# A hybrid decoder layer on one core: the gate columns of its input projection, from one product per tile and half to pairs of tiles with seven block products over both halves

## The chip, the core and the metric

The kernel runs on one core of one Trainium2 chip. TensorE (PE) multiplies matrices into PSUM; VectorE (DVE), ScalarE (ACT) and GpSimd (POOL) do the elementwise work, GpSimd without access to PSUM; SyncE (SP) issues most of the transfers between the chip's memory and SBUF, POOL and ACT issue the others. The metric is the device time of one launch in microseconds (us), lower is better.

## The reference, cut to what matters

```python
h = rms_norm(x, norm_w)                       # x (1024 positions, 2048)
proj = h @ w_in                               # 8704 columns
q, k, v, a_gate, u, z, g_a, g_s = jnp.split(proj, split_pts, axis=-1)   # a_gate, u, z 1024 wide; g_a, g_s 2048
attn = sliding_window_attention(rms(q), rms(k), v, sinks)               # window 128
y_a = (attn * jax.nn.silu(a_gate)) @ w_attn_proj
y_ssm = jax.nn.gelu(s5_ssm(u, ...))           # a diagonal complex scan over the positions
glu_a, glu_b = jnp.split(y_ssm @ w_glu + b_glu, 2, axis=-1)
y_s = (glu_a * jax.nn.sigmoid(glu_b) * jax.nn.silu(z)) @ w_ssm_proj
merged = jax.nn.sigmoid(g_a) * y_a + jax.nn.sigmoid(g_s) * y_s
return x + merged @ w_out
```

The gate columns are `a_gate`, `z`, `g_a` and `g_s`: 6144 of the 8704. All data are fp32.

## The kernel before, in words

Everything is held transposed: channels on the 128 partitions, positions along the free axis, in two halves of 512 positions (h = 0 and 1; `TH` is 512). A weight tile `win(n)` is 2048 rows by 128 columns and is loaded as two blocks of 8 x 128 rows (`wraw`, 128x1024 elements, 512 KB). For fp32 accuracy every operand is split into a rounded part and a rest: `split` (lines 81 and 82) makes `hi` by a copy on ACT and `lo` by a subtraction on DVE. A block product takes 8 row tiles of 128, three matmuls for each (hi by hi, hi by lo, lo by hi): 24 matmuls of 128x128 by 128x512, added up in one PSUM bank.

The input projection has 68 weight tiles: 0 to 11 for k, v and q, 12 to 19 for u, 20 to 27 for z (`gate`), 28 to 35 for the attention gate (`gate` with `by`), 36 to 51 for g_a and 52 to 67 for g_s (`sigmoids`). `proj` (line 111) makes each tile for each half by itself, so a tile costs two block products per half, four in all, and its weights are loaded and split twice. A gate's bank is multiplied with `rstd` on DVE (L176, L186), goes through the sigmoid on ACT (L177, L187) and is stored by POOL's queue (L178, L193). `build_raw` makes the split operand `hh`/`hl` of a half: 16 pairs of an ACT and a DVE instruction (L143, L144).

The later products (GLU, attention output, SSM output, final output) already use a scheme with seven block products for the eight of a 2 x 2 block matrix. For GLU, attention and SSM `four` does it for a pair of weight tiles; for the final output `out1`, `out2`, `out3` do it in three walks over the tiles, with intermediate results in memory. Sums of weight blocks are made by `wadd` on POOL (L856).

Work is emitted by generators: `drive` runs one and, after each of its steps, `pull` advances the side generators in `sides` by their rate (`spawn(gen, rate)`); `drain` finishes them. A scheduler then orders the instructions of each engine by priority on its own estimate of when they become ready, and each engine and each queue runs its list in order. Tiles with one tag of a pool share its `bufs` buffers; a tile waits until one is free. The split weights have two buffers, the loaded blocks (`raw`) two.

The order of the stages: u and z of half 0 beside the SSM's tables (`ssm_prep`); k, v, q of half 0; u, k, v, q of half 1 beside attention of half 0; z and half of g_a of half 1 beside attention of half 1; the other gates of half 1, then a_gate and g_a of half 0, beside `ssm` (the scan: in four batches of 16 groups, each with DVE steps in `step`, POOL products of its tables, L661, and px and py matmuls, L706, L753, L754); g_s of half 0 beside the input sums of the GLU; then the later products.

The shape of the scheme in the kernel before, for one product of the second walk of the final output:

```python
r1, r2, r3 = rring(wout(8 + j, 0)), rring(wout(8 + j, 1)), rring(wout(j, 0))
w1, w2 = wsum(), wsum()
wadd(w1, r1, r2)
wadd(w2, r3, w1)
t = wsplit(w2)
y = bank(1)
product(y, t, 0, ops[6])
```

## Time and profile before

| what | value |
|---|---|
| time, median of 3 runs | 2614.22 us (2613.48 to 2615.66) |
| profiled execution: time, span | 2613.01 us, 2611.2 us |
| mean granted TensorE clock | 0.981 |
| busy: PE, DVE, ACT, POOL | 2480.6, 1654.7, 916.9, 917.3 us |
| PE instructions (matmuls and transposes) | 11012 |
| bytes moved, mean rate | 438.55 MB, 168 GB/s |

The span is from the first to the last instruction. A busy share is an average over stages of different kinds; the windows by stage show them apart. A granted clock below 1 is a mean over stretches at 2.4 GHz and at 1.2 GHz. DVE, ACT and POOL times count instructions from start to end, waits for a shared memory port among them.

### The profile page before, as it was taken

How to read it: one execution, taken by the hardware profiler on the slowest of the kernel's cores; microseconds unless marked ns; L12 is line 12 of the kernel's file. 1: busy time of each engine (PE TensorE's matmuls, PEld its weight loads, DVE VectorE, ACT ScalarE, POOL GpSimd, SP SyncE). 2: the span in 40 equal slices, each digit the busy share in tenths (PEclk: the TensorE clock that was granted, in tenths of full speed). 3: DMA queues.
4: the chain of work that ended last, by engine and by line, in shares of the span. 5: the costliest groups of instructions: out<-in, count | busy, mean ns of one | idle time of the engine just before them, and what ended most of it. 6: DMA issues, size and time to landing. Idle time of an engine off the chain costs nothing. (4 is left out here: it accounts for less than half of the span.)

```text
span 2611.2 us, 30785 instructions
## 1 busy us (share of the span) xinstructions
PE 2480.6 (95%) x11012; PEld 2016.8 (77%) x11012; DVE 1654.7 (63%) x2294; ACT 916.9 (35%) x1378; POOL 917.3 (35%) x715
## 2 busy tenths in 40 slices
PE   7999999999999998899999989999999999899997
PEld 5878887788878777787777868887877877678886
DVE  7995557984776287948586243226687686744542
ACT  5332454453666223131332232223352231233311
POOL 4110014350444534132120230004547656514466
PEclk9999999999999998999999999999999999999999
DMA  6543343223333745445464674336358677797765
GB/s 206 191 139 109 96 141 105 84 83 97 97 95 103 217 129 135 152 129 157 133 168 135 210 259 156 121 121 202 120 191 282 211 257 234 246 313 270 226 218 181
DMA packets 195609, 438.55 MB, mean 168 GB/s; under 512 B 41312, under 2 KB 53632, under 8 KB 195456
## 3 DMA queue, kind: packets, MB, share of 16 engines
q1 hardware_dynamic: 159680, 344.14, 43.6%
q0 software_dynamic: 19504, 63.08, 6.4%
q10 hardware_dynamic: 16272, 29.38, 2.9%
q8 instruction: 86, 1.41, 0.2%
q14 instruction: 67, 0.55, 0.1%
HBM read 341.73 MB, written 94.77 MB: 167 GB/s over the span
## 5 line engine op out<-in xcount | busy, mean ns | idle before, releaser
L121 PE MATMUL ps<-hh,whi 128*128 128x512 f32 x2144 | 851.3, 397 | 13.7 <-ACT whi L81 9.7
L122 PE MATMUL ps<-hl,whi 128*128 128x512 f32 x2144 | 844.5, 394 | 0.8 <-DVE hl L144 0.8
L82 DVE TENSOR_TENSOR wlo<-wraw,whi 128x1024 fp32r<-128x1024 f32 (+1 forms) x344 | 448.6, 1306 | 455.3 <-ACT whi L81 216.9
L125 PE MATMUL ps<-hh,wlo 128*128 128x512 f32 x2144 | 549.8, 396 | 32.0 <-DVE wlo L82 32.0
L81 ACT CAST whi<-wraw 128x1024 fp32r<-128x1024 f32 (+1 forms) x344 | 348.4, 1014 | 627.4 <-PE ps L122 301.3
L125 PEld LDWEIGHTS ps<-hh,wlo 128*128 128x128 f32 x2144 | 404.7, 190 | 124.6 <-DVE wlo L82 39.5
L121 PEld LDWEIGHTS ps<-hh,whi 128*128 128x128 f32 x2144 | 407.2, 190 | 108.5 <-ACT whi L81 17.1
L122 PEld LDWEIGHTS ps<-hl,whi 128*128 128x128 f32 x2144 | 407.1, 190 | 86.7 <-DVE hl L144 2.1
L82 DVE TENSOR_TENSOR wlo<-ws,whi 128x1024 fp32r<-128x1024 f32 x80 | 118.9, 1488 | 127.1 <-ACT whi L81 93.7
L81 ACT CAST whi<-ws 128x1024 fp32r<-128x1024 f32 x80 | 84.0, 1051 | 307.5 <-POOL ws L856 116.7
L856 POOL TENSOR_TENSOR ws<-wraw 128x512 f32<-128x512 f32 (+1 forms) x72 | 136.5, 1896 | 135.6 <-DVE wlo L82 103.3
L421 POOL TENSOR_TENSOR pa<-ph,c_mct 128x512 fp32r<-128x512 f32 x32 | 43.1, 1347 | 253.8 <-ACT ph L81 253.6
L178 POOL DMA_DIRECT2D gsd<-sg x32 | 17.5, 547 | 274.9 <-ACT sg L177 274.9
L177 ACT ACTIVATE sg<-sg 128x512 f32<-128x512 f32 x64 | 40.5, 632 | 198.1 <-DVE sg L176 198.0
L661 DVE TENSOR_TENSOR v<-X,be 64x16 f32<-64x16 f32 (+2 forms) x192 | 91.9, 479 | 2.8
L402 ACT ACTIVATE scs<-scs,m,rq 128x128 f32<-128x128 f32 x128 | 61.8, 484 | 63.9 <-DVE m L396 63.9
L1001 POOL TENSOR_TENSOR mt<-mt,pa 128x512 f32<-128x512 f32 x32 | 57.0, 1782 | 76.9 <-DMA pa<-pd 24.3
L178 POOL DMA_DIRECT2D gd<-sg x32 | 17.8, 556 | 170.6 <-ACT sg L177 163.5
L862 PE MATMUL psm<-q4h,whi 128*128 128x512 f32 x160 | 67.6, 422 | 4.0 <-DVE mt L996 2.7
L862 PE MATMUL psm<-q1h,whi 128*128 128x512 f32 x160 | 64.4, 403 | 6.1 <-ACT whi L81 6.1
L863 PE MATMUL psm<-q4l,whi 128*128 128x512 f32 x160 | 66.2, 414 | 0.0
L862 PE MATMUL psm<-q2h,whi 128*128 128x512 f32 x160 | 62.6, 392 | 3.1 <-ACT qa L893 3.1
(343 smaller groups left out, 4187.8 us busy)
## 6 DMA issues: line engine op xcount, KB each, us to landing
wraw<-w_in SPq DMA_DIRECT2D x268, 512.0 KB, 3.6
wraw<-w_out SPq DMA_DIRECT2D x72, 512.0 KB, 5.2
x<-xT SPq DMA_DIRECT2D x96, 256.0 KB, 4.0
gd<-sg POOLq DMA_DIRECT2D x32, 256.0 KB, 3.9
gsd<-sg POOLq DMA_DIRECT2D x32, 256.0 KB, 2.9
wraw<-w_glu SPq DMA_DIRECT2D x16, 512.0 KB, 4.3
wraw<-w_attn SPq DMA_DIRECT2D x16, 512.0 KB, 5.1
sga<-gd SPq DMA_DIRECT2D x32, 256.0 KB, 4.3
```

The source lines that it names most:

```text
L81: S.copy(hi, src)
L82: V.tensor_tensor(lo, src if src2 is None else src2, hi.bitcast(F32), op=ALU.subtract)
L121: PE.matmul(ps, hi[:, kk, :], rh[kt], start=(kt == 0), stop=False)
L122: PE.matmul(ps, hi[:, kk, :], rl[kt], start=False, stop=False)
L125: PE.matmul(ps, lo[:, kk, :], rh[kt], start=False, stop=(kt == last))
L402: S.activation(sc[:, r, :], sc[:, r, :], AF.Exp, bias=m4[:, r:r + 1], scale=RQ[h, p][:, b, 2 * r + e:2 * r + e + 1], accum_out=den[:, r:r ...
L421: G.tensor_tensor(a, ph.bitcast(F32), mb, op=ALU.mult)
L661: (eng or V).tensor_tensor(o, a, b, op=op)
L856: G.tensor_tensor(o, a, b, op=ADD)
L862: PE.matmul(ps, hi[:, c0 + k, :], rh, start=(first and k == 0), stop=False, skip_group_check=True)
L863: PE.matmul(ps, hi[:, c0 + k, :], rl, start=False, stop=False, skip_group_check=True)
L1001: G.tensor_tensor(t, t, p, op=ADD)
```

## The change

All 48 gate tiles are made in 24 pairs of tiles (`PAIRS`; kinds a = g_a, s = g_s, z, o = a_gate) over both halves at once, with seven block products to a pair, in three walks over the pairs. The products of a walk use operands that are the same for all pairs, so each walk holds only two or three of the seven operands (eight split row tiles each). The operands that are sums over halves and row blocks are made by `inputs`, from x normalised anew, and stored in `HD`; `operands` loads and splits them. Walk 1 writes `QG[0]`, walk 2 reads it and writes `QG[1]` and `QG[2]`, walk 3 reads these. The weights of walk 2 and 3 are sums of blocks, made in place in the loaded blocks by POOL.

Half 1 goes first now: the prologue and `uproj(1)` use half 1, then half 0's operands are built (`build_raw(0)`), then u, k, v, q of half 0. Half 1's operands are then built with `rstd` in them (`build_h`), and its banks are copied or go to the sigmoid without a factor. The first eight pairs of walk 1 run ahead of k, v, q of half 1 beside attention of half 0, twelve more beside attention of half 1 and `inputs`, the last four beside the start of the SSM. The SSM runs beside walk 2 and twenty pairs of walk 3, with one buffer each for uq, X, ct, c1, c2 and the scan's temporaries, and with tables of 16 groups instead of 64. The loaded blocks get four buffers in one pool (`RAW`), where `rring` took two from each of two pools. The sums of the GLU's inputs run beside pairs 20 to 22 of walk 3, its operands are loaded beside pair 23, and the sums of the attention gate's inputs move beside the GLU.

```diff
+RAW = 4
+    HD = dp.tile([5, 8, 128, TH], F32, name="hd")
+    QG = [dp.tile([24, 128, TH], F32, name=f"qg{n}") for n in range(3)]
-        raw = wp.tile([128, KC, 128], F32, tag="raw", name="wraw")
+        raw = wp.tile([128, KC, 128], F32, tag="raw", bufs=RAW, name="wraw")
...
     def evac(ps, out, h):
-        V.tensor_tensor(out, ps, rstd[h], op=ALU.mult)
+        if h:
+            S.copy(out, ps)
+        else:
+            V.tensor_tensor(out, ps, rstd[h], op=ALU.mult)
...
-            uq = tl((128, GB, NCH), "uq", 2)
+            uq = tl((128, GB, NCH), "uq", 1)
-            X = tl((128, GB, NCH + 1), "X", 2)
+            X = tl((128, GB, NCH + 1), "X", 1)
-                v1 = tl((128, 840), f"v1{bt % 2}")[:, 0:n]
+                v1 = tl((128, 840), "v1")[:, 0:n]
...
+    PAIRS = ([("a", j, 36 + j, 44 + j, j, 8 + j) for j in range(8)] +
+             [("s", j, 52 + j, 60 + j, j, 8 + j) for j in range(8)] +
+             [("z", j, 20 + j, 24 + j, j, 4 + j) for j in range(4)] +
+             [("o", j, 28 + j, 32 + j, j, 4 + j) for j in range(4)])
+    def inputs():
+        def block(k, h, tag):
+            t = load_x(k, h, tag=tag)
+            V.scalar_tensor_tensor(t, t, nw[:, k:k + 1], rstd[h], op0=ALU.mult, op1=ALU.mult)
+            return t
+        for k in range(8):
+            b12, b11 = block(k, 0, "x"), block(k, 1, "x")
+            G.tensor_tensor(b11, b11, b12, op=SUB)
+            nc.gpsimd.dma_start(HD[0, k], b11)
+            yield
+            b22 = block(8 + k, 0, "ld")
+            nc.sync.dma_start(HD[4, k], b22)
+            G.tensor_tensor(b12, b12, b22, op=SUB)
+            nc.gpsimd.dma_start(HD[2, k], b12)
+            G.tensor_tensor(b11, b11, b22, op=ADD)
+            nc.gpsimd.dma_start(HD[1, k], b11)
+            yield
+            b21 = block(8 + k, 1, "ld")
+            G.tensor_tensor(b21, b21, b11, op=SUB)
+            nc.gpsimd.dma_start(HD[3, k], b21)
+            yield
+    def gate(kind, n, h, ps, op=None, other=None):
+        dst = {"a": GD, "s": GSD, "z": ZD, "o": AGD}[kind][h][n]
+        x = ps
+        if op is not None:
+            x = et("gx")
+            V.tensor_tensor(x, ps, other, op=op)
+        if kind in "as":
+            sg = et("sg") if op is None else x
+            S.activation(sg, x, AF.Sigmoid)
+        else:
+            sg = et("sg")
+            S.activation(sg, x, AF.Sigmoid)
+            V.tensor_tensor(sg, x, sg, op=MUL)
+            if kind == "o":
+                o = ld(AOD[h][n], "go")
+                G.tensor_tensor(sg, sg, o, op=MUL)
+        nc.gpsimd.dma_start(dst, sg)
+    def gates1(ops, a, b):
+        for p in range(a, b):
+            kind, _, na, nb, ia, ib = PAIRS[p]
+            with tc.high_priority(offset=200):
+                t1 = wsplit(rring(wq(na, 0)))
+            x = bank(0)
+            product(x, t1, 0, ops[1])
+            q = et("qa")
+            S.copy(q, x)
+            nc.gpsimd.dma_start(QG[0][p], q)
+            yield
+            with tc.high_priority(offset=200):
+                t2 = wsplit(rring(wq(na, 1)))
+            product(x, t2, 0, ops[2], first=False)
+            gate(kind, ia, 1, x)
+            yield
+    def gates2(ops, a, b):
+        for p in range(a, b):
+            kind, _, na, nb, ia, ib = PAIRS[p]
+            q = ld(QG[0][p], "qa")
+            with tc.high_priority(offset=200):
+                w5, r, w6 = rring(wq(nb, 0)), rring(wq(nb, 1)), rring(wq(na, 0))
+                wadd(w5, w5, r)
+                wadd(w6, w6, w5)
+                t = wsplit(w6)
+            y = bank(0)
+            product(y, t, 0, ops[6])
+            v = et("qb")
+            V.tensor_tensor(v, q, y, op=SUB)
+            nc.gpsimd.dma_start(QG[1][p], v)
+            yield
+            with tc.high_priority(offset=200):
+                t = wsplit(w5)
+            y = bank(0)
+            product(y, t, 0, ops[5])
+            e = et("qe")
+            V.tensor_tensor(e, y, v, op=ADD)
+            nc.gpsimd.dma_start(QG[2][p], e)
+            yield
+    def gates3(ops, a, b):
...
+                    w[7], r, w[4], w[3] = rring(wq(na, 0)), rring(wq(nb, 0)), rring(wq(nb, 1)), rring(wq(na, 1))
+                    wadd(w[7], w[7], r)
...
+                    wadd(w[3], w[3], w[4])
+                    wadd(w[3], w[3], w[7])
+                    t = wsplit(w[3])
+                y = bank(0)
+                product(y, t, 0, ops[3])
+                gate(kind, ia, 0, y, ADD, e)
...
+            product(z, t, 0, ops[7])
+            gate(kind, ib, 0, z, SUB, e)
...
+            product(z, t, 0, ops[4], first=False)
+            gate(kind, ib, 1, z, SUB, v)
...
-    spawn(stats1(), 1.0)
+    spawn(stats0(), 1.4)
     spawn(ssm_prep(b0, p0), 1.0)
-    drive(uproj(0, hh0, hl0, done, 4))
-    drive(gate(20, ZD[0], hh0, hl0, rstd[0]))
+    drive(uproj(1, hh0, hl0, done, 4))
+    hh, hl = build_raw(0)
+    drive(uproj(0, hh, hl))
...
-    drive(kvq(0, hh0, hl0))
+    drive(kvq(0, hh, hl))
     spawn(attention(0), 2.2)
-    hh, hl = build_raw(1)
-    drive(uproj(1, hh, hl))
+    hh, hl = build_h(1)
+    hu = list(zip(hh, hl))
+    og = {1: hu[0:8], 2: hu[8:16]}
+    drive(gates1(og, 0, 8))
     drive(kvq(1, hh, hl))
     drain()
-    spawn(attention(1), 2.2)
-    drive(gate(20, ZD[1], hh, hl, rstd[1]))
-    drive(sigmoids(36, GD[1], hh, hl, rstd[1], 0, 8))
+    spawn(attention(1), 2.8)
+    spawn(inputs(), 1.0)
+    drive(gates1(og, 8, 20))
     drain()
...
-    spawn(ssm(bp, pp), 0.8)
-    drive(sigmoids(36, GD[1], hh, hl, rstd[1], 8, 16))
-    drive(gate(28, AGD[1], hh, hl, rstd[1], AOD[1]))
-    drive(sigmoids(52, GSD[1], hh, hl, rstd[1], 0, 16))
-    hh, hl = build_raw(0)
-    drive(gate(28, AGD[0], hh, hl, rstd[0], AOD[0]))
-    drive(sigmoids(36, GD[0], hh, hl, rstd[0], 0, 16))
+    spawn(ssm(bp, pp), 0.7)
+    operands((6,), 1.5)
+    drive(gates1(og, 20, 23))
+    drain2()
+    operands((5,), 4.0)
+    drive(gates1(og, 23, 24))
+    drain2()
+    operands((3,), 1.5)
+    drive(gates2(og, 0, 23))
+    drain2()
+    operands((7, 4), 4.0)
+    drive(gates2(og, 23, 24))
+    drain2()
+    drive(gates3(og, 0, 20))
     drain()
...
     spawn(combos(By, CBD["y"], 4), 0.5)
-    drive(sigmoids(52, GSD[0], hh, hl, rstd[0], 0, 8))
+    drive(gates3(og, 20, 23))
     drain()
-    spawn(load_ops(oy, source(By, CBD["y"]), 4, ORDER), 0.5)
-    spawn(combos(Ba, CBD["a"], 4), 0.3)
-    drive(sigmoids(52, GSD[0], hh, hl, rstd[0], 8, 16))
+    n = load_ops(oy, source(By, CBD["y"]), 4, ORDER)
+    next(n)
+    spawn(n, 5.0)
+    drive(gates3(og, 23, 24))
     drain()
+    spawn(combos(Ba, CBD["a"], 4), 0.2)
     stage(glu, oy, load_ops(oa, source(Ba, CBD["a"]), 4, ORDER))
```

## Rows read from the trace of the kernel before

**Rows 1.** Page: busy time, share of the span, instructions of PE and DVE.

```profile
PE 2480.6 (95%) x11012; PEld 2016.8 (77%) x11012; DVE 1654.7 (63%) x2294; ACT 916.9 (35%) x1378; POOL 917.3 (35%) x715
```

**Rows 2.** Windows: length, busy us (instructions) PE PEld DVE ACT POOL, clock, DMA share, GB/s.

```profile
605.00:851.00 246.00, 241.95 (x1130) 197.41 (x1129) 165.08 (x240) 149.28 (x282) 98.33 (x83) 0.99 0.31 99
851.00:1594.00 743.00, 681.72 (x3072) 558.08 (x3071) 452.30 (x726) 206.71 (x247) 206.19 (x169) 0.97 0.56 167
1594.00:1780.00 186.00, 186.00 (x823) 154.12 (x822) 59.39 (x58) 48.42 (x54) 16.79 (x22) 1.00 0.38 121
2300.00:2612.00 312.00, 296.50 (x1296) 243.93 (x1295) 137.36 (x142) 79.58 (x100) 156.38 (x98) 0.98 0.72 240
```

**Rows 3.** Tile sg on DVE, 1594 to 1780: count, ns min/median/max, first and last start.

```profile
L176 DVE TENSOR_TENSOR sg<-ps,rstd x18: 678/684/685, 1594.4 to 1779.8; 128x512 f32<-128x512 f32 x18
```

**Rows 4.** PE's waits, 851 to 1594: us in total, times, longest.

```profile
PE ps L125 <- DVE wlo L82: 32.0, 15, 4.8
PE px L706 <- POOL bm L661: 13.0, 2, 6.5
```

**Rows 5.** Groups of instructions by form, whole span: busy us, mean ns, idle before.

```profile
L856 POOL TENSOR_TENSOR ws<-wraw 128x1024 f32<-128x1024 f32 x24 | 61.3, 2554 | 60.6 <-DVE wlo L82 28.3 <-DMA qb<-qd 12.6 <-DMA wraw<-w_out 7.9
L856 POOL TENSOR_TENSOR ws<-ws 128x1024 f32<-128x1024 f32 x8 | 19.4, 2430 | 0.2
L856 POOL TENSOR_TENSOR ws<-wraw,ws 128x1024 f32<-128x1024 f32 x8 | 19.1, 2393 | 22.2 <-issue 14.7 <-DMA wraw<-w_out 3.8 <-DVE wlo L82 3.6
L81 ACT CAST whi<-wraw 128x1024 fp32r<-128x1024 f32 x316 | 331.2, 1049 | 574.5 <-PE ps L122 301.3 <-DMA wraw<-w_in 137.9 <-PE psm L863 37.5
```

**Rows 6.** The same on POOL, 851 to 1594.

```profile
L661 POOL TENSOR_TENSOR bm<-bm,bmu 128x512 f32<-128x512 f32 x16 | 25.4, 1587 | 0.5
...
L178 POOL DMA_DIRECT2D gd<-sg x24 | 13.3, 552 | 128.7 <-ACT sg L177 121.7 <-issue 7.0
...
L661 POOL TENSOR_TENSOR bmu<-pwi,bim 128x512 f32<-128x512 f32 x8 | 12.2, 1523 | 13.0 <-DMA bim<-sBiT 7.9 <-DMA bre<-sBrT 5.0
```

**Rows 7.** The same on DVE, 851 to 1594.

```profile
L82 DVE TENSOR_TENSOR wlo<-wraw,whi 128x1024 fp32r<-128x1024 f32 x113 | 158.9, 1408 | 179.3 <-ACT whi L81 105.7 <-PE ps L125 62.4 <-DMA c<-sC 7.0
L661 DVE TENSOR_TENSOR v<-X,be 64x256 f32<-64x256 f32 x56 | 44.3, 790 | 0.8
...
L661 DVE TENSOR_TENSOR v<-v,v 128x840 f32<-128x840 f32 x8 | 8.2, 1024 | 0.0
```

**Rows 8.** DVE's timeline at the first scan: start us, us, engine line.

```profile
929.57 3.02 DVE L661 TENSOR_TENSOR v<-X,be 64x256 f32<-64x256 f32 x2
...
934.00 2.06 DVE L661 TENSOR_TENSOR X<-X,v 128x256 f32<-128x256 f32 x1
...
942.51 1.28 DVE L661 TENSOR_TENSOR v<-X,be 64x256 f32<-64x256 f32 x2
...
944.29 0.67 DVE L661 TENSOR_TENSOR X<-X,v 128x256 f32<-128x256 f32 x1
```

**Rows 9.** POOL's timeline there: the last of six table products, and what follows it.

```profile
937.14 1.46 POOL L661 TENSOR_TENSOR bm<-bm,bmu 128x512 f32<-128x512 f32 x1
950.10 0.58 POOL L178 DMA_DIRECT2D gd<-sg  x1 [11.50 <-ACT sg L177]
```

**Rows 10.** Windows: eight of 100 us with DVE over 70%; two of them, their sum.

```profile
2000.00:2100.00 100.00, 99.39 (x437) 81.41 (x436) 70.42 (x77) 30.57 (x41) 59.38 (x43) 1.00 0.74 238
...
2200.00:2300.00 100.00, 85.52 (x341) 67.28 (x340) 71.56 (x81) 27.07 (x37) 52.84 (x33) 0.93 0.77 248
sum 800.00, PE 731.86 PEld 591.33 DVE 619.35 ACT 234.47 POOL 344.31; mean PE 91.48 PEld 73.92 DVE 77.42 ACT 29.31 POOL 43.04
```

**Rows 11.** Groups on POOL, 605 to 851.

```profile
L421 POOL TENSOR_TENSOR pa<-ph,c_mpt 128x512 fp32r<-128x512 f32 x16 | 23.5, 1468 | 0.0
```

**Rows 12.** DMA issues: KB each, median us from issue to landing.

```profile
wraw<-w_in SPq DMA_DIRECT2D x268, 512.0 KB, 3.6
```

**Rows 13.** Groups on DVE, 335 to 375.

```profile
L144 DVE SCALAR_TENSOR_TENSOR hl<-x,nw,hh 128x512 fp32r<-128x512 f32 x16 | 11.4, 746 | 8.0 <-ACT hh L143 8.0
```

More of the change, by code (lines that the diff above doesn't have):

```diff
@@ L1130, in drain, with drain2 @@
         sides.clear()
+    def drain2():
+        for s in list(sides):
+            if s[2] >= 1.5:
+                for _ in s[0]:
+                    pass
+                sides.remove(s)
     def drive(gen):
```

154 lines of the change are left out of this document (87 added, 67 removed).

## The prediction, on record before the changed kernel ran

> **What bounds the kernel now.** I read the page's busy line first: PE is busy 95% of the span, no other engine over 63% [rows 1], so the count of matmuls is what has to fall. Then the windows by stage, to see where PE is not at its limit. From 1594 to 1780, with no side work, PE is busy all the time at granted clock 1.00 [rows 2], and the 18 evacuations of that stage start from 1594.4 to 1779.8 [rows 3]: 17 steps in 185.4 us, 10.91 us for two block products, **5.453 us for a product of 24 matmuls**. Next the stage beside the SSM, 851 to 1594: 56 tiles, 112 products, 610.7 us of its 743. PE is idle for 743 - 681.7 = 61.3 us there and the clock is 0.97 [rows 2], some 22 us; the remaining 49 us are the SSM's own matmuls. The waits of PE in it are mostly for the rest of the weight split, on DVE, and for the SSM's table products on POOL [rows 4]. So there is one bound, PE, and one stage that loses 83 us (61 + 22) to its helpers.
>
> **The matmuls removed.** The 48 gate tiles take 48 x 4 = 192 products, the 24 pairs take 24 x 7 = 168. 24 products less, 576 matmuls: 24 x 5.453 = **-130.9 us**. This comes off PE's own path, nothing covers it, and it is the whole of what the change can win outside the waits. The rest asks how much the helpers take back.
>
> **The walks beside the SSM.** It now stands beside 4 pairs of walk 1, all of walk 2 and 20 pairs of walk 3: 8 + 48 + 60 = 116 products, 632.5 us, and with its own 49 us 681.5.
>
> POOL: two sums for a pair in walk 2, three in walk 3, 108 here, of 128x1024. The three groups of such sums mean 2.495 us [rows 5], so 269 us. The SSM's tables are eight groups from 25.4 down to 12.2 us, 138 in all [rows 6]. Stores: 12 + 48 + 60 = 120 at 0.552 us [rows 6], 66. With the four products with the attention's output some 7. That is 480 of 681.5, 70%, where POOL had 206 of 743, 28% [rows 2].
>
> DVE: 116 splits at 1.408 us, 163; 108 banks combined at 0.684 [rows 3], 74; 16 gate products at the same, 11; the split of 40 operand tiles, each half as large as a weight split, 0.7, so 28; the SSM's steps, twelve groups from 44.3 down to 8.2 us, 211 [rows 7]. 487 us, 71%; before, 452 of 743, 61% [rows 2].
>
> So both helpers are nearer their limit while PE gives them less time. What this costs PE can only be bounded. Nearest from below is the final output, which makes the same sums in the same three walks without an SSM: it loses 15.5 of 312 us and 2% of the clock [rows 2], 7%, 48 us here. The eight windows of 100 us in which DVE is over 70% busy, as it will be, lose 8.5% of PE on the mean, and their clocks lie from 0.93 to 1.00 [rows 10]; with 3.5% for that, 12%: 681.5 / 0.88 = 774, 93 us. The worst of them loses 14.5% and 7% [rows 10]: 681.5 / 0.785 = 868, 187 us. I take 105, a little above the mean, because POOL was at 43% in the eight on the mean and will be at 70%. Against 83 before: **+22** (-35 to +104).
>
> SSM with single buffers: a batch's uq and X are loaded and cleared only when the batch before has made its last py matmul. Side steps come slower too (0.7 for 0.8 of a product), 116 x 0.7 = 81 steps for some 70 needed, so there are about 16 products, 87 us, of reserve before the drain, and then 12 products that need nothing of the SSM. I cost it at nothing; its price if that is gone is the remaining scan beyond 87 + 65 us.
>
> SP's queue: walk 3 issues four blocks and two intermediate tiles for 3 products, 2.6 MB in 16.4 us, 160 GB/s, about the 167 that this stage moved already [rows 2], at 3.6 us from issue to landing [rows 12]. Four buffers of raw blocks instead of two start them earlier. Nothing. On POOL's queue a store now waits for its sigmoid or combination with sums behind it; POOL stood idle 128.7 us in front of 24 stores [rows 6], so this waiting takes time that the sums want. It is inside the 105.
>
> **Walk 1 beside attention of half 1.** Before, 32 products (174.5 us) and 71.5 us of attention and waits made 246 [rows 2]; now 24 products, so 202 us. POOL: attention's mask products are four groups like the one shown, 88 us together [rows 11]; `inputs` adds 32 sums of about 1.55 us (one of that size on POOL is 1.587 [rows 6]), 50, and 32 stores, 18; the gates' 24 stores 13, attention's 5: 174 of 202. DVE: 165 [rows 2] less 8 splits (10) and all the products with `rstd` (18), plus 32 normalising instructions of 0.746 [rows 13] to 1.0 us, say 28: 165, 82%. Sigmoids and exponentials already shared ACT in this stage, at 61% [rows 2]. The cover if this runs late is the 8 products of pairs 20 to 23, 44 us, that need nothing of it; without that cover the 12% of above would take 202 / 0.88 - 202 = 28. Less the 5 us lost in this stage now: 0 to +23, I take **+8**.
>
> **Building half 1.** Half 1's operands take two DVE instructions for each tile, 0.746 [rows 13] and about 0.7, so 23 us where 12 stood. PE can only start on what is built: 0 to +11, I take **+6**. The new build of half 0 between the two u projections replaces one that stood in the SSM's stage. In exchange, walk 1 loses its DVE evacuations, which were hidden.
>
> **Entry into the GLU.** Its 28 operand tiles (7.3 MB, 30 us at the final stage's 240 GB/s [rows 2]; 20 us of DVE) must now be loaded in pair 23, 16.4 us, and during the first GLU tile, 19 us; they had 16 products before. Sums of the attention gate's inputs come beside the GLU as well. 0 to +20; I take **+10**. The order of the halves, the second build and the side rates of the first stages otherwise move equal work.
>
> **Sum.** -130.9 + 22 + 8 + 6 + 10 = -85. The profiled execution took 2613.0, its span 2611.2; the median of the runs is 1.2 above it. 2613.0 - 85 + 1.2 = **2529 us**.
>
> **Rivals.**
>
> *Nothing is given back* (chance 0.22). The sums of walk 2 and 3 have the form that the final output's have, where PE is busy 95%; four raw buffers prefetch deeper; and the 13 us for POOL's tables and the loss in the SSM's stage may shrink when the scan is spread thinner. With the other terms at zero and the stage's loss the same it is 2614 - 131 = 2483; at the lower bound 2450. Against it: a busier POOL beside the same scan.
>
> *Contention makes DVE the bound of the walks* (0.18). While POOL makes its table products, two scan instructions take 3.02 us and one 2.06; with POOL silent after 938.6 the same take 1.28 and 0.67 [rows 8, 9], 5.08 against 1.95, 2.6 times. POOL's sums and tables cover 407 of 681.5 us, 60%. The 256-wide steps, four groups of which the longest is shown [rows 7], 101 us together, were taken mostly with POOL silent; at 60% cover the factor 1 + 0.6 x 1.6 = 1.96 makes them 198 at most. The splits and wide steps have less to lose, some 40. DVE then needs 487 + 97 + 40 = 624, and at the 77.4% at which it ran in the eight windows [rows 10] the stage is 806, at 71.6% 872: 125 to 190 us lost, where 83 were. With 24 of other terms, 2614 - 131 + 42 + 24 = 2549, up to 2614, middle 2582. For it speaks that the sums are moved onto the one engine that slows the scan; against it, that 2000 to 2100 holds 59% of POOL and 70% of DVE with PE at 99.4% [rows 10].
>
> The Trainium skill (GPSIMD Engine Reference, 1. Specifications) says that GpSimd's SBUF interfaces are shared with VectorE and contend with VectorE instructions that have two SBUF inputs. By that rule every split and scan step is exposed, and the slower end of this rival is the likelier; the trace agrees on the scan, with 2.06 against 0.67 us.
>
> *Walk 2's chain becomes the bound* (0.15), which is slower than before. Place: sums are made in the raw blocks themselves, so a block is held until it is split, and a pair needs three of four. If buffers come free in turn, the second load of a pair waits for the split of the pair before: 1.05 [rows 5] + 1.41 us [rows 7], then the load 3.6 [rows 12], two sums 5.0, and ACT's half of the split 1.05: 12.1 us where a pair has 10.9. 1.2 us for a pair, and with a table product of POOL (1.5 to 2.7 us) ahead of each sum up to 5.4. 24 x 5.4 = 130 us: 2614 - 131 + 46 + 130 = 2659. It decides from (131 - 46) / 24 = 3.5 us for a pair. Against it: if a load takes whichever buffer is free, the third load starts 3 us before the product of sums, its sums are done 3 us into it, and the split has until the next such product, 6 us of slack.
>
> **Chances and range.** Forecast 0.45 (2505 to 2555), the three rivals 0.22, 0.18 and 0.15. The range for 8 in 10 goes from **2470 to 2612**: below it lies the lower end of the first rival, above it the third. A measurement of this kernel tells 0.2%, 5 us, from no change. Faster by more: 0.45 + 0.22 + 0.17 of the second rival = 0.84; within: 0.03, from the edges of the second and third; slower: 0.13.
>
> **What would show it.** PE's instructions fall by 576 to 10436. Products in walks with no stall are 10.9 us for two. In the walks beside the SSM, DVE over 70% and POOL near 70% busy, PE's waits led by wlo on DVE; the 256-wide scan groups well over the 790 ns of [rows 7] if contention is real. Were waits for whi behind POOL sums to lead in walk 2, at a steady step over 12 us for a pair, the chain rival holds. PE idle at the end of the stage with scan steps alone would show that single buffers cost what I put at nothing. A time under 2490 would say that helpers had room that my 71% and 70% deny; over 2610, that one of them is the bound.

## The result and the profile after

The changed kernel takes **2741.98 us** (median of 4 runs, 2740.12 to 2750.47) against 2614.94 (4 runs, 2613.48 to 2617.65): a ratio of **1.049**, 95% interval 1.0467 to 1.0515. It is slower by 127 us where 85 us less were forecast, and the time lies outside the range (2470 to 2612). All rows of the kernel after are from the longest of its four executions, 2750.47 us.

The page's busy line answers to [rows 1]. PE's instructions fell by exactly 576 and its busy time by 51 us, but its share fell from 95% to 88%; DVE rose by 227 us, POOL by 418. The columns are busy time, share of the span and instructions.

```profile
PE 2429.5 (88%) x10436; PEld 1956.9 (71%) x10436; DVE 1882.0 (68%) x2354; ACT 929.2 (34%) x1428; POOL 1334.9 (49%) x987
```

The windows by stage of the kernel after (columns as in [rows 2]): first stages; the keys, values and queries of half 0; walk 1 beside attention of half 0; its rest beside attention of half 1; walks 2 and 3 beside the SSM; the entry into the GLU; the rest.

```profile
0.00:240.00 240.00, 211.62 (x931) 165.73 (x932) 194.00 (x319) 87.62 (x124) 58.10 (x67) 0.95 0.56 182
240.00:400.00 160.00, 148.49 (x650) 121.44 (x648) 91.91 (x150) 64.79 (x121) 7.96 (x6) 0.92 0.25 79
400.00:760.00 360.00, 310.19 (x1312) 244.48 (x1312) 270.51 (x360) 174.08 (x343) 164.42 (x146) 0.89 0.44 143
760.00:991.00 231.00, 209.76 (x938) 169.17 (x937) 128.57 (x169) 120.94 (x222) 119.56 (x109) 0.95 0.43 139
991.00:1740.00 749.00, 601.63 (x2570) 487.01 (x2571) 550.38 (x699) 178.84 (x216) 405.53 (x248) 0.90 0.59 178
1740.00:1940.00 200.00, 175.88 (x729) 141.18 (x728) 120.13 (x115) 62.53 (x86) 124.91 (x95) 0.93 0.77 253
1940.00:2749.00 809.00, 771.92 (x3312) 627.84 (x3311) 526.51 (x547) 240.35 (x319) 454.42 (x318) 0.98 0.73 240
```

The stage beside the SSM is as long as before (749 us for 743 in [rows 2]) with 502 matmuls less in it. PE is idle there for 147 us instead of 61, and the granted clock is 0.90 instead of 0.97. Lower stretches come behind waits: after the wait of 11.6 us at 147 (below) the clock granted from 151 to 164 was 0.50, that is 1.2 GHz. No helper is full: DVE 73%, POOL 54%. The stage is also not the one that was planned: the last four pairs of walk 1 ran before 991, and some five of its pairs of walk 3 come after 1740, so it holds 93 products instead of 116.

To add idle time and clock without counting anything twice, I took from the trace, for every matmul, the time to the start of the next one, less the median of that time for its line and shape, and summed these differences by stage. In us:

| stage (before / after) | before | after | more | forecast |
|---|---|---|---|---|
| first stages, 0 to 240 | 16 | 36 | +20 | 0 |
| 240 to 851 / 240 to 991: attention, building half 1, walk 1 | 28 | 131 | +103 | +14 |
| beside the SSM, 851 to 1594 / 991 to 1740 | 90 | 204 | +114 | +22 |
| to the GLU, 1594 to 1780 / 1740 to 1940 | 0 | 35 | +35 | +10 |
| the rest | 58 | 51 | -7 | 0 |
| sum | 192 | 456 | +264 | +46 |

264 - 131 for the matmuls removed = +133; the spans differ by 2748.7 - 2611.2 = 137.5. So the table accounts for the result, and no term of it is a PE instruction. Two terms of the same size make most of it: the stage beside the SSM loses 92 us more than was forecast, the stages of attention 89 more.

Who is waited for in the largest term: PE's waits in 991 to 1740 (us in total, times, longest), to be read against [rows 4], where wlo had 32.0 us.

```profile
PE psm L855 <- DVE wlo L86: 64.1, 21, 8.0
PE psm L852 <- ACT whi L85: 63.6, 14, 13.1
PE py L737 <- DMA p<-ptd: 8.6, 1, 8.6
PE py L737 <- DMA c<-sC: 7.4, 1, 7.4
```

In the kernel before, whi had 9.7 us (851 to 1594):

```profile
PE ps L121 <- ACT whi L81: 9.7, 6, 3.8
```

And the DVE groups that answer to [rows 7], in the same stretch (busy us, mean ns, idle before): the split's mean went from 1408 to 1783 ns, the 64x256 scan step from 790 to 974.

```profile
L86 DVE TENSOR_TENSOR wlo<-wraw,whi 128x1024 fp32r<-128x1024 f32 x93 | 165.7, 1783 | 153.3 <-ACT whi L85 88.3 <-PE psm L855 53.9 <-issue 7.2
L644 DVE TENSOR_TENSOR v<-X,be 64x256 f32<-64x256 f32 x56 | 54.6, 974 | 0.8
L644 DVE TENSOR_TENSOR v<-X,be 64x16 f32<-64x16 f32 x120 | 34.2, 285 | 1.7
```

A mean hides how this comes about. The same splits in the kernel before (851 to 1594), the kernel after (991 to 1740) and c1 (below; 851 to 1682): ns min/median/max, first and last start.

```profile
L82 DVE TENSOR_TENSOR wlo<-wraw,whi x113: 1204/1225/3300, 849.4 to 1593.2; 128x1024 fp32r<-128x1024 f32 x113
L86 DVE TENSOR_TENSOR wlo<-wraw,whi x93: 1203/1225/9475, 1004.9 to 1736.1; 128x1024 fp32r<-128x1024 f32 x93
L82 DVE TENSOR_TENSOR wlo<-wraw,whi x114: 1208/1226/16632, 854.0 to 1680.9; 128x1024 fp32r<-128x1024 f32 x114
```

Half of the splits take 1.2 us as ever, and a few take very long. I sorted them by whether a sum or table product of POOL ran during them: in the kernel after, the 47 without one take at most 1.24 us, the 46 with one 2.36 us on the mean. The scan's steps fare the same, and a split stands behind them in DVE's order. One of PE's longest waits for wlo (start us, us; the hi part was ready at 1034.36):

```profile
1037.40 2.41 POOL L846 TENSOR_TENSOR wraw<-wraw 128x1024 f32<-128x1024 f32 x1
1037.55 3.88 DVE L644 TENSOR_TENSOR v<-X,al 128x256 f32<-128x256 f32 x1
1039.76 1.27 POOL L644 TENSOR_TENSOR bm<-bm,bmu 128x512 f32<-128x512 f32 x1
...
1043.81 0.61 DVE L644 TENSOR_TENSOR v<-X,al 128x256 f32<-128x256 f32 x1
...
1046.29 1.22 DVE L86 TENSOR_TENSOR wlo<-wraw,whi 128x1024 fp32r<-128x1024 f32 x1
1047.56 3.78 PE L855 MATMUL psm<-q6h,wlo 128*128 128x512 f32 x8 [7.46 <-DVE wlo L86]
```

The scan step that takes 0.61 us alone starts just behind a sum and ends 0.4 us after POOL's two instructions, at 1041.43; the split that PE waits for takes its usual time and starts late. Of PE's 21 waits for wlo most are of this kind: the splits that ended them are over their 1.2 us by 19 us in all, and the waits are 64. From the end of the hi part to the start of the rest 2.4 us pass on the mean in the kernel before, 4.9 in the kernel after, 3.6 in c1 and 0.6 in a3, where there is no scan (waits for a free buffer among them).

An evacuation, which has one input in PSUM, keeps its time beside the same sums:

```profile
L1142 DVE TENSOR_TENSOR gx<-psm,qe x29: 673/679/684, 1420.2 to 1737.2; 128x512 f32<-128x512 f32 x29
```

The POOL group that is new there, by which the experiments go on:

```profile
L846 POOL TENSOR_TENSOR wraw<-wraw 128x1024 f32<-128x1024 f32 x93 | 237.1, 2550 | 207.3 <-DMA wraw<-w_in 153.0 <-DVE gx L1142 16.3 <-issue 10.3
```

### The profile page after: what moved, and what is told of

The parts are those of the page before. It is cut to its first block, busy times and chain, and to the rows that moved or that the text cites. A ratio compares the mean times of both kernels' runs of the same rounds, so it can differ in the third digit from the quotient of the medians.

```text
span 2748.7 us, 30805 instructions
## 1 busy us (share of the span) xinstructions
PE 2429.5 (88%) x10436; PEld 1956.9 (71%) x10436; DVE 1882.0 (68%) x2354; ACT 929.2 (34%) x1428; POOL 1334.9 (49%) x987
## 5 line engine op out<-in xcount | busy, mean ns | idle before, releaser
L846 POOL TENSOR_TENSOR wraw<-wraw 128x1024 f32<-128x1024 f32 x120 | 304.1, 2535 | 229.7 <-DMA wraw<-w_in 171.0
L125 PE MATMUL ps<-hh,whi 128*128 128x512 f32 x608 | 242.8, 400 | 13.0 <-DVE ut L185 11.6
L126 PE MATMUL ps<-hl,whi 128*128 128x512 f32 x608 | 242.5, 399 | 3.8 <-DVE hl L148 3.8
L852 PE MATMUL psm<-hh,whi 128*128 128x512 f32 x384 | 158.8, 413 | 5.3 <-ACT qa L1166 4.0
L853 PE MATMUL psm<-hl,whi 128*128 128x512 f32 x384 | 156.6, 408 | 2.9 <-DVE hl L86 2.9
L129 PE MATMUL ps<-hh,wlo 128*128 128x512 f32 x608 | 157.0, 396 | 0.2 <-DVE wlo L86 0.2
L125 PEld LDWEIGHTS ps<-hh,whi 128*128 128x128 f32 x608 | 116.9, 192 | 39.0 <-issue 12.3
L126 PEld LDWEIGHTS ps<-hl,whi 128*128 128x128 f32 x608 | 116.9, 192 | 32.5 <-DVE hl L148 7.1
L852 PE MATMUL psm<-q7h,whi 128*128 128x512 f32 x352 | 137.3, 390 | 1.9 <-ACT whi L85 1.9
L129 PEld LDWEIGHTS ps<-hh,wlo 128*128 128x128 f32 x608 | 115.5, 191 | 25.7 <-DVE wlo L86 0.6
```

What stands on the lines that cost most here:

```text
L125: PE.matmul(ps, hi[:, kk, :], rh[kt], start=(kt == 0), stop=False)
L126: PE.matmul(ps, hi[:, kk, :], rl[kt], start=False, stop=False)
L129: PE.matmul(ps, lo[:, kk, :], rh[kt], start=False, stop=(kt == last))
L846: G.tensor_tensor(o, a, b, op=ADD)
L852: PE.matmul(ps, hi[:, c0 + k, :], rh, start=(first and k == 0), stop=False, skip_group_check=True)
L853: PE.matmul(ps, hi[:, c0 + k, :], rl, start=False, stop=False, skip_group_check=True)
```

## Experiments

Theory: POOL's sums slow DVE's scan and splits. Rivals: a chain from block to sum to split to product; single SSM buffers and the new order; DVE's amount of work. Apart from that, what the attention stages and the first stages lose. All are variants of the kernel after but one, of the kernel before. Times are single runs unless told. One kernel's runs lie up to 16 us apart (seven runs of the kernel before beside f1), and the kernel before took 2607 to 2621 us beside the single runs, so a difference under some 16 us between single runs decides nothing.

**Sums left out (a1).** The products take the loaded blocks as they are.

```
-                wadd(w5, w5, r)
-                wadd(w6, w6, w5)
...
-                    wadd(w[7], w[7], r)
...
-                    wadd(w[3], w[3], w[4])
-                    wadd(w[3], w[3], w[7])
```

> The weight sums of walk 2 and 3 are left out; the blocks are loaded and the products take them unsummed. The changed kernel lost about 200 us in walk 2 and 3 beside the SSM (991 to 1740). Theory 'sums' (the chain of load, sum, split in one set of four buffers, or POOL's sums slowing VectorE): the time falls by 90 to 150 us, to 2590 to 2650. Rival 'scan' (VectorE is too full with the SSM's steps and two evacuations for each pair, whoever makes the sums): it falls by less than 40, to 2700 to 2740.

2616.09 us, 126 less. Its window of the stage: DVE's busy time falls by 138 us although no DVE instruction was removed (694 in the window, 699 in that of the kernel after).

```profile
985.00:1620.00 635.00, 564.36 (x2532) 464.73 (x2533) 412.61 (x694) 178.79 (x212) 171.87 (x155) 0.93 0.70 211
```

The DVE groups there, their means back near [rows 7]:

```profile
L86 DVE TENSOR_TENSOR wlo<-wraw,whi 128x1024 fp32r<-128x1024 f32 x91 | 125.8, 1384 | 178.8 <-ACT whi L85 115.2 <-PE psm L855 41.6 <-issue 19.3
L644 DVE TENSOR_TENSOR v<-X,be 64x16 f32<-64x16 f32 x120 | 21.1, 176 | 1.7
```

**The same sums where nobody reads them (a2).** As many POOL instructions of the same size, on a block that is loaded and not used; the products are unsummed.

```
-                wadd(w5, w5, r)
-                wadd(w6, w6, w5)
+                wadd(r, r, r)
+                wadd(r, r, r)
...
```

> As many sums of the same size on POOL, but all on a loaded block that no product reads; the products take unsummed blocks. POOL is as busy as before and contends as before, but no split waits for a sum. Theory 'chain': it falls nearly as far as without sums, 80 to 140 us, to 2600 to 2660. Theory 'contention on the memory port': it stays within 30 us of 2742.

2713.6 us: 97.5 more than without sums and 28 less than with real ones. No split waits for these sums, so of the 126 us some 98 come with POOL's work alone and at most 28 with the chain behind real sums. That the 98 are contention this run does not show by itself: the block is held until its sums are done, POOL's stores stand behind them, and with one block as both inputs such a sum took 2.13 us instead of 2.55. c1 has neither block nor chain. The window:

```profile
991.00:1710.00 719.00, 597.02 (x2568) 484.35 (x2569) 523.68 (x699) 180.76 (x216) 369.48 (x253) 0.91 0.61 188
```

The split in it:

```profile
L86 DVE TENSOR_TENSOR wlo<-wraw,whi 128x1024 fp32r<-128x1024 f32 x93 | 158.1, 1702 | 171.7 <-ACT whi L85 126.9 <-PE psm L855 24.2 <-issue 10.7
```

**No scan (a3).** The SSM's scan and its products are left out; the GLU reads the attention's output.

```
-    spawn(ssm(bp, pp), 0.7)
...
```

> The SSM's scan is left out (the GLU reads the attention output in its place). 49 us of its matmuls go in any case. 'Chain': the walks keep most of their loss, the time falls by 50 to 110, to 2630 to 2690, and a pair of walk 2 stays over 12 us. 'Contention' and 'scan': the walks run at about 10.9 us for a pair, the time falls by 170 to 240, to 2500 to 2570.

2562.41 us, 180 less, 49 of which are the scan's own matmuls. Its window:

```profile
985.00:1600.00 615.00, 563.18 (x2384) 453.53 (x2383) 272.60 (x238) 149.40 (x180) 315.51 (x213) 0.98 0.62 210
```

The split in it:

```profile
L86 DVE TENSOR_TENSOR wlo<-wraw,whi 128x1024 fp32r<-128x1024 f32 x101 | 167.4, 1660 | 277.4 <-ACT whi L85 196.8 <-PE psm L855 77.2 <-issue 3.4
```

The tile qb, of which there is one in each pair of walk 2 (ns min/median/max, first and last start):

```profile
L1187 DVE TENSOR_TENSOR qb<-qa,psm x24: 672/680/689, 1007.9 to 1271.5; 128x512 f32<-128x512 f32 x24
```

23 steps in 263.6 us, 11.5 for a pair. The same tile in the kernel after:

```profile
L1187 DVE TENSOR_TENSOR qb<-qa,psm x24: 669/679/695, 1019.2 to 1384.0; 128x512 f32<-128x512 f32 x24
```

15.9 for a pair. So with every sum in the chain, but no scan, a pair of walk 2 takes 0.6 us over the 10.9 of undisturbed products. The splits are nearly as slow on the mean as with the scan (1660 ns), but the longest takes 3.4 us, DVE is at 44%, and PE waits for wlo 2.8 us in all.

The chain is not free, though. In walk 3 a pair takes 19.2 us in a3 (72 banks from 1297.2 to 1752.5), where three undisturbed products are 16.4; it is 19.0 in a1 and 22.0 in the kernel after. By the measure of the table a3's stage still loses 74 us, and PE's waits in it are for whi:

```profile
PE psm L852 <- ACT whi L85: 44.2, 30, 4.4
```

So neither the sums without the scan (74 us lost) nor the scan without the sums (102 in a1) loses what both do together (204).

**POOL work of that size in the kernel before (c1).** No walk, no chain, double SSM buffers; three multiplications on a block of zeros (128x440, 128x880, 128x440) are added on POOL for each gate tile beside the scan.

```
+            d = dum[0]
+            nc.gpsimd.tensor_tensor(d[:, 0], d[:, 0], sg[:, 0:440], op=ALU.mult)
+            nc.gpsimd.tensor_tensor(d, d, d, op=ALU.mult)
+            nc.gpsimd.tensor_tensor(d[:, 0], d[:, 0], d[:, 1], op=ALU.mult)
             nc.gpsimd.dma_start(dst[n], sg)
```

> The kernel before, with POOL work of the size of the pair sums added beside the scan: for each of the 56 gate tiles of the SSM's stage three multiplications on a block of zeros (128x440, 128x880, 128x440), some 250 us on POOL, whose result nothing uses; nothing waits for them but the release of one gate buffer, by the first of them. Contention theory: DVE's time in that stage grows from 452 us to 540 or more, wlo and the 64x256 scan steps become slower as they did in the kernel after (1.22 to 1.78 us, 790 to 974 ns), and the time goes up by 50 to 100 us, to 2660 to 2710. Rival (the loss comes from the walks' order, their chain from block to sum to split, and from single SSM buffers): none of these is here, so the time stays within 15 us of 2614 and DVE near 455 us.

2701.29 us against 2612.40, **+89 us** from 250 us of POOL work that no result needs. Its window (the stage now ends at 1682):

```profile
851.00:1682.00 831.00, 715.23 (x3119) 579.85 (x3118) 562.27 (x705) 201.23 (x236) 409.42 (x298) 0.93 0.45 128
```

The wait of PE that leads in it:

```profile
PE ps L125 <- DVE wlo L82: 90.3, 27, 8.2
```

Two groups on DVE and the longest of the added ones on POOL:

```profile
L82 DVE TENSOR_TENSOR wlo<-wraw,whi 128x1024 fp32r<-128x1024 f32 x114 | 211.9, 1861 | 225.1 <-ACT whi L81 137.6 <-PE ps L125 81.7 <-issue 4.0
L672 DVE TENSOR_TENSOR v<-X,be 64x16 f32<-64x16 f32 x120 | 31.7, 265 | 1.7
...
L177 POOL TENSOR_TENSOR dum<-dum 128x880 f32<-128x880 f32 x55 | 98.4, 1790 | 1.2
```

DVE goes from 452 ([rows 2]) to 562 us with much the same instructions (705 in the window, 726 before), the splits from 1408 to 1861 ns, and PE's wait for wlo from 32.0 ([rows 4]) to 90.3 us. Its longest split, from 906.70, takes 16.6 us beside a row of POOL instructions without a pause up to 922.25 and ends 1.08 us after it; PE waits 7.3 us for it. A gate's store stands behind the added work, but no wait of DVE in this stage is for a gate's buffer. By the measure of the table the stage loses 167 us where it lost 90. This is a like amount of POOL work without anything else of the change; the rival of order, chain and buffers expected no effect.

**The sums on DVE (b3).**

```
+    def vadd(o, a, b):
+        V.tensor_tensor(o, a, b, op=ADD)
...
-                wadd(w5, w5, r)
+                vadd(w5, w5, r)
...
```

> The 120 weight sums of walk 2 and 3 are made on VectorE instead of POOL: about 1.2 us each without contention, 145 us more instructions there. 'Contention' (POOL's sums slow what VectorE does in the walks by 143 us: 550 busy with them, 407 without): VectorE is about as busy as now, 540 to 570 us, the time stays within 30 us of 2742. 'VectorE too full' (no contention, only work): 60 us or more slower, over 2800. If sums on VectorE cost less than what POOL's cost it: under 2710.

2690.92 us, 51 less, though DVE has the sums' work in addition: its busy time in the stage is 543 us, less than the 550 it had without them. The window:

```profile
985.00:1690.00 705.00, 587.11 (x2534) 474.18 (x2534) 543.14 (x791) 172.61 (x209) 184.50 (x159) 0.92 0.64 194
```

The sums and the splits on DVE, 1.48 us for a sum where POOL took 2.55 (the share of DVE is higher than in the kernel after, 77%, and by the measure of the table the stage loses less, 159 us):

```profile
L1176 DVE TENSOR_TENSOR wraw<-wraw 128x1024 f32<-128x1024 f32 x94 | 139.5, 1484 | 134.2 <-DMA wraw<-w_in 130.3 <-DMA pwr<-pwd 3.5
L86 DVE TENSOR_TENSOR wlo<-wraw,whi 128x1024 fp32r<-128x1024 f32 x92 | 129.5, 1407 | 19.1 <-PE psm L855 14.8 <-ACT whi L85 3.5
```

**The sums by DMA (b4)**, as accumulating transfers on POOL's queue.

```
+        nc.gpsimd.dma_start(o, a, accum_op=ADD)
...
```

> The sums are made by accumulating transfers (POOL's queue, from memory or from the other block in SBUF) into the loaded blocks; no engine adds. Same results, no POOL sums beside the scan, 24 loads of walk 2 and 24 of walk 3 turned into accumulating ones, 72 transfers more. 'Contention': the walks go as without sums, time 2610 to 2650. 'Chain' (a split waits for the sums): an accumulating transfer takes longer than a sum of 2.5 us, so it would be slower than 2742.

2743.44 us, no gain. DVE falls to 436 us and a split to 1401 ns, so most of the contention is gone, but the DMA engines are at 90%, and such a sum lands 5.7 us after its issue (from a block in SBUF) or 7.8 (from the weights). The window:

```profile
985.00:1740.00 755.00, 624.51 (x2710) 510.84 (x2709) 435.72 (x714) 188.15 (x226) 270.83 (x276) 0.91 0.90 234
```

What binds it now is not settled. ACT waits 196.9 us for the sums, but in the kernel after it waited as long for POOL's (199.1 us in 991 to 1400), and idle time of ACT alone costs nothing. PE's waits are spread over whi, wlo (31.6 us) and the SSM's transfers:

```profile
PE psm L852 <- ACT whi L85: 32.6, 13, 7.7
PE py L737 <- DMA tz<-kd: 29.6, 3, 13.1
```

The accumulating transfers (KB each, median us from issue to landing):

```profile
wraw<-wraw POOLq DMA_DIRECT2D x57, 512.0 KB, 5.7
wraw<-w_in POOLq DMA_DIRECT2D x41, 512.0 KB, 7.8
```

**The attention stages: inputs left out (a4), own buffers (b1).** a4 leaves out the half sums of the normalised input and loads x as operand. b1 takes the shared buffers ("ev") of three tiles away.

```
-    spawn(inputs(), 1.0)
...
```

```
-            t = sp.tile([128, TH], F32, tag="ev", name="hn")
+            t = x
...
-            sq = sp.tile([8, TH], F32, tag="ev", name="rqs")
+            sq = atp.tile([128, TH], F32, tag="wk", bufs=4, name="rqs")[0:8]
...
-        S.copy(ol, po[64:128])
+        S.copy(ao[z:z + 64], po[64:128].rearrange("d (r t) -> d r t", r=4))
```

> The side work that makes the summed operands (32 loads, 32 steps on VectorE, 32 sums on POOL, 40 stores) is left out; the operands are loaded from x. In the changed kernel it ran from 433 to 624, beside attention of half 0, and the stage from 240 to 760 lost some 85 us more than before. Theory 'inputs ran beside the wrong stage': the time falls by 40 to 80, to 2660 to 2700. Rival 'attention's own buffers and the build of half 1 make the loss': it falls by less than 20.

> Three small tiles are taken out of the shared 'ev' buffers: half 1's build normalises in place in x, rqs moves to 'wk', and attention's ol is added in place in ao. In the changed kernel the build of half 1 (hn) waited in 'ev' until the last q tile was through (404.1), while PE had only attention to do from 366 to 405, and the same happened at 700 to 760. Theory 'shared buffers hold the build and attention back': the build starts before 375, the stages from 240 to 991 lose 40 to 80 us less, time 2660 to 2700. Rival 'attention and inputs simply fill VectorE there': less than 20 us, 2722 or more.

a4 2717.35 us (-25), b1 2724.32 (-18, hardly over the noise); both fall between their two theories. By the measure of the table a4 loses 35 us less in 400 to 760 and some 8 more behind it, b1 22 less in 240 to 760. `inputs`, written for attention of half 1, ran in large part beside attention of half 0: its stores run from 433 to 624 us in the kernel after, since the scheduler takes what it reckons to be ready. What PE waits for in 400 to 760 of the kernel after is the attention's own work on DVE, which [rows 2] had at 67% of such a stage and which is at 75% now:

```profile
PE psc L363 <- DVE scs L374: 18.8, 6, 9.2
PE pt L394 <- DVE scs L390: 9.0, 3, 3.5
```

**Statistics of half 0 earlier (b2).** `spawn(stats0(), 4.0)` for 1.4.

> The statistics of half 0 run as side work at 4.0 steps a product instead of 1.4. In the changed kernel u of half 0 has its matmuls done and waits for rstd of half 0 (PE waits 11.6 us at 147 for a bank of PSUM, the clock falls to half after it). Theory 'late rstd': the wait at 147 goes, 12 to 22 us less, 2720 to 2730. Rival 'the SSM tables on VectorE are the limit there': the wait moves, less than 6 us.

2750.85 us, no gain. The wait of the bank for half 0's rstd,

```profile
PE ps L125 <- DVE ut L185: 11.6, 1, 11.6
```

fell to 6.0 us, but the last u tile came only 1.4 us earlier: DVE is at 81% in 0 to 240 in both.

**Combined (c2), and everything named left out (c3).** c2 has the sums on DVE, own buffers, and half 0's u copied out of the bank by ACT (`early=8`). c3 has no sums, no inputs, own buffers and `early=8`.

> The kernel after with three changes together: the 120 sums of walks 2 and 3 on DVE, the three shared evacuation buffers of the attention stages replaced by buffers of their own use, and half 0's u tiles copied out of the bank by ACT, so that no bank waits for rstd of half 0. If the costs add: 2742 - 51 (sums on DVE) - 18 (own buffers) - 12 to 24 (the 11.6 us wait for rstd and the half clock around it) = 2649 to 2661. Rival (the stalls replace each other, DVE being the common bound): over 2680. Faster than the kernel before only if they help each other by another 35 us.

> The kernel after with everything taken out that the single runs priced: no sums in walks 2 and 3, no blocks made from half sums of the normalised input (x itself is loaded as operand), own buffers, half 0's u out of the bank by ACT. The scan stays. If the prices add: 2742 - 126 - 25 - 18 - 12 to 24 = 2549 to 2561. What is left over 2483 (the time with 576 matmuls fewer and no other loss) is then the price of attention and scan themselves under the new order, 66 to 78 us. Rival (helpers' work was all of the loss): under 2520.

c2 2644.06 us and c3 2541.47, 5 and 8 under the least that the single gains add up to: within the noise they add. By the measure of the table c3 still loses 251 us, 59 over the kernel before: 86 beside the scan (90 before), 83 from 240 to 960 (28 before), 21 at the start (16), 11 at the entry into the GLU (0), 50 in the rest (58). So without the sums the walks lose no more than the old stage, and what stays is in the attention stages. There 49 of the 83 lie between 760 and 960, in the second half of it where attention ends and walk 2 begins (DVE is busy 39.5 us of 920 to 960, and the first qb starts at 938.6); 400 to 760 is nearly clean, at a granted clock of 0.99.

**First sums by DMA (c4).** Of c2, 48 of 120 sums by the DMA that loads the second block.

> As the combined kernel, but the first sum of a pair in walks 2 and 3 (48 of 120) is made by the DMA that loads its second block (it adds to the block already there), the other 72 on DVE. No bytes are added. Contention and DVE load theory: DVE loses 48 sums of some 1.2 us, 58 us, in the walks, PE gets half of it back: 25 to 30 us under the combined kernel, 2620 to 2635. Rival (with sums by DMA the landing of 7.8 us seen in the run with all sums by DMA becomes the chain): no faster than the combined kernel, PE's waits for whi behind wraw.

2675.02 us, 31 over c2, though DVE is 496 us busy in 730 where it had 533 in 700. The rival had the time right but not the wait: those for wlo lead with 58.3 us, whi has 14.5. Why it is slower stays open.

**Chain or queue on DVE: order of the products (d1, d2, d3), banks ahead of the scan (e1, e2).** In d1 and d3 a pair's product with the two-block sum comes first, in d2 the scan is also spread; e1 and e2 put v, e and gx ahead in DVE's order.

```
-                wadd(w6, w6, w5)
-                t = wsplit(w6)
...
+            for m in (6, 5) if p == 0 else (5, 6):
...
```

```
+                with tc.high_priority(offset=200):
+                    V.tensor_tensor(v, q, y, op=SUB)
```

> The combined kernel (2644) with the two products of a pair in walk 2 in the other order from the second pair on: first the product with the sum of two blocks, then the one with the sum of three, so that one sum stands before each split instead of two before the first and none before the second. The work of every engine is the same. Chain theory: walk 2's stretch loses 20 to 40 us less, 2604 to 2624. DVE's total as the cause: within 8 us of 2644.

> The same with side steps of the SSM at 0.62 of a product instead of 0.7, so that the scan reaches over all of walks 2 and 3. If DVE's total per product sets the loss, 5 to 15 us under the kernel with the order changed alone; if the order in which the scan is offered does not matter to when it runs, within 5 us of it; if the scan then ends after the walks, 10 to 30 us over it.

> The kernel after with nothing but the changed order of the two products in walk 2; the sums stay on POOL. If two sums in a row before a split are a chain of their own (5 us on POOL): 20 to 50 us under 2742. If POOL's sums act through DVE alone, whose work and contention stay: within 10 us of 2742.

> The combined kernel with the products of walk 2 in the other order, and the combinations of banks in walks 2 and 3 (v, e, gx) put ahead of the scan in DVE's order. If order is the cause: the 47 us of waits for qb go, 2661 falls to 2615 to 2635. If DVE's total is the cause: the waits come back at wlo or whi, 2645 to 2665.

> The combined kernel (2644, products of walk 2 in their old order) with the same priority for the combinations of banks. If order is the cause: 2615 to 2635. If DVE's total is the cause: within 8 us of 2644.

d1 2660.93 (c2 2644), d2 2659.66, d3 2733.55 (after 2742), e1 2643.82, e2 2629.72. No gain from the order shows in either kernel, nor from a thinner scan. e2 falls into the span of "order", but 14 us under c2 is within the noise; in e1 the waits for qb that were to go are still 42.1 us. PE's waits in the walks of c2,

```profile
PE psm L854 <- DVE wlo L86: 53.0, 22, 11.3
PE psm L851 <- DVE qb L1189: 14.5, 2, 14.1
```

and of d1

```profile
PE psm L851 <- DVE qb L1195: 46.9, 12, 10.0
PE psm L854 <- DVE wlo L86: 22.7, 12, 5.5
```

show one wait turned into another: 67.5 and 69.6 us in the two rows together, both for DVE. Where the work for a product stands in DVE's order moves the waits about and does not lessen them: all waits of PE for DVE in these stretches are 75 us in c2 and 99 in d1.

**The best of them (f1), three rounds.** e2 with the last four pairs' sums back on POOL and walk 1's copies ahead on ACT.

> The combined kernel with the combinations of banks ahead of the scan (2630), and two small edits: the sums of the last four pairs of walk 3, made after the scan has ended, go back to POOL (12 sums of some 1.4 us off DVE, which was the later of the two there), and walk 1's copies out of the bank on ACT are put ahead. If both help, 5 to 15 us less, 2615 to 2625, the kernel before within 0.5%; if neither does, 2630 plus or minus 5.

2641.25 us (4 runs, 2634.38 to 2644.80) against 2609.81 (7 runs, 2602.77 to 2618.57): ratio 1.0109, interval 1.0073 to 1.0144. 100 us better than the kernel after, and still slower than before. It lies where c2 does, so e2's 2630, which was not repeated by itself, is not confirmed as a step below c2.

## Why the prediction was wrong

Four terms came out above their bounds, and two of them carry the miss. Either alone, added to 2529, leaves the range: 2621 with the first, 2618 with the second.

*The matmuls removed, -130.9*: right as far as the trace shows it. 576 instructions fewer, with 10.9 us for two products where nothing disturbs ([rows 3]; 11.5 in a3).

*The walks beside the SSM, +22 (bounds -35 to +104)*: **this is the first step that failed**; it was +114, above its upper bound. I read the loss off windows of the kernel before by DVE's share of busy time. DVE's share came as forecast, 73% for 71% (POOL's did not, 54% for 70%), and the loss was 204 us where I took 105, in a stretch of 93 products where I had counted 116. So the share does not give the loss: b3 has 77% and loses 159, c1 has 68% and loses 167. The mistake is that a DVE instruction's duration is not its own: beside POOL's sums much the same instructions take 550 us (413 in a1, without sums), and what grows are the single instructions that meet one of POOL's, among them the scan steps that stand before a split. That no helper was full says nothing against it. Of the stage's loss over the old one, a1 leaves 12 us; a2 puts some 98 of the 126 that it gains to POOL's work without a chain, and c1 makes +77 by such work alone. The Trainium skill (GPSIMD Engine Reference, 1. Specifications), named in the prediction for one rival, says that GpSimd's SBUF interfaces contend with VectorE instructions that have two SBUF inputs. The traces agree: splits and scan steps have two and grow, evacuations have one in PSUM and stay at 0.68 us.

*The nearest row from below*, the final output, was no likeness: it makes such sums without a scan. Without the scan a3 loses 74 us in 615, not far from the 48 that this row gave; with the scan it is 204.

*The rival "contention makes DVE the bound of the walks"* had the cause and the place. It was priced at up to 190 us lost, and 204 came, but not by its sum: it made DVE's need 624 us and let DVE run full, and DVE was busy 550 us at 73%. It gave splits and wide steps "some 40" for what c1 shows as 51 in the splits alone ((1861 - 1408) ns x 113). Its time, 2549 to 2614, failed because the other terms were small in it.

*The rival "walk 2's chain"* gave the nearest time, 2659, and one of its signs came, with 15.9 us for a pair; the waits for whi came second and did not lead (63.6 us to 64.1). Its cause carries little of it: 0.6 us for a pair of walk 2 in a3, at most 28 us between a2 and the kernel after, and no gain clear of the noise when one sum instead of two stands before a split (d3). That its time came nearest is luck.

*Single buffers of the SSM, nothing*: not tried by themselves, as double ones find no room beside the walks. PE's waits before py, the products that end a batch of the scan, are 25 us in the kernel after (16 of them are shown above, for the tables p and c of 16 groups), 18 in a1, 2 in the kernel before and 5 in c1, which has its buffers and tables. So some 20 us lie in a term that was put at nothing; a1, whose walks lose 102 us with single buffers and no sums where the old stage lost 90, bounds it.

*Walk 1 beside attention, +8 (0 to +23), and building half 1, +6 (0 to +11)*: **this is the second step that failed**; together +103. I had counted POOL's and DVE's busy shares again, and placed `inputs` where the text spawns it, not where it ran. Runs price 25 of it (`inputs`) and 18 (buffers); c3, without both, still loses 55 us more than before there, mostly where attention ends and walk 2 begins. The remainder stays open. In the kernel after, attention's waits are short and many, and the granted clock is 0.89 in 400 to 760 (0.98 to 0.99 before), but what the clock alone costs I did not separate.

*Entry into the GLU, +10 (0 to +20)*: +35. It goes with the sums of the last nine or ten pairs of walk 3, which run in it: 10 and 11 without sums (a1, c3), 17 and 23 with sums on DVE (b3, c2), 32 with sums on POOL and no scan (a3).

*The order of the halves, nothing*: +20. A bank of half 0 waits 11.6 us for its rstd; with ACT copying it out (c2) the stage loses 22 instead of 36.

*What would show it*: "over 2610, that one of them is the bound" pointed to the right place, but no helper was full: two busy ones shared something.

## What to carry to other kernels

Before moving work onto an idle engine, ask what it does to the durations of the busy one beside it: run the kernel as it is with dummy work of that size there (c1 is one run and gave +77 of the stage's +114). In this kernel a trade of PE work for POOL work beside a DVE scan was a trade against DVE. Busy times from uncontended rows do not say how long the same instructions take beside another engine (413 and 550 us here), so look at the longest instruction of a group and not at its mean alone. Engine shares under 80% were no proof of room where the work of one product passes through three engines in order.

## What the runs showed of the hardware

- Sums on POOL lengthen DVE's instructions with two inputs in SBUF beside them: splits on the mean from 1408 to 1783 ns (after) and 1861 (c1), 64x16 scan steps from 176 to 285 and 265 ns. The median of the splits stays at 1225; instructions that read PSUM (gx, qb) stay at 679 to 682 ns.
- A split that starts beside a row of POOL instructions without a pause can last until the row ends: 9.5 us in the kernel after and 16.6 us in c1, each ending 1.1 us after the row. Splits that meet no sum or table product of POOL take 1.2 us in all six kernels sorted (before, after, a1, a3, b3, c1).
- The sum itself is faster on DVE beside the scan (1.48 us) than on POOL (2.55).
- A 512 KB accumulating DMA landed after 5.7 us from SBUF and 7.8 us from HBM in b4, where plain loads of that size beside it took 5.8; plain loads took 4.5 in the kernel after.
- The mean granted clock fell from 0.981 to 0.932, most in the two stages that lose most (0.89 in 400 to 760, 0.90 in 991 to 1740); after one wait of 11.6 us it was 0.50 for 13 us.
